# HGRN2 recurrence by halvings for two heads at once, forget and query projections in seven products

## The chip, the cores and the metric

The kernel runs on one core of a Trainium2 chip. The metric is device time in microseconds (us): the median of three runs.

## The reference, cut to what matters

One layer of a trunk on 512 frames of width 1024, in float32. After an RMSNorm `h`, one projection by `w_in` gives eight column groups: `zu`, `zv` (gMLP, 512 each), `zq`, `zf`, `zi`, `zo` (recurrence, 1024 each) and two gates of 1024.

```python
log_f = log_sigmoid(zf); k = sigmoid(-zf); q = silu(zq)       # 8 heads of 128
# S_t = diag(f_t) S_(t-1) + k_t v_t^T ;  o_t = S_t^T q_t, v = zi
o = rmsnorm(o, norm_g) * silu(zo)
mix = sigmoid(g_a) * (gmlp @ w_up_a) + sigmoid(g_b) * (o @ w_up_b)
x = x + mix @ w_out
x = rmsnorm(x + square(relu(rmsnorm(x) @ w_ff1)) @ w_ff2)
```

Within a group of 128 frames the recurrence is a causal 128x128 score matrix per head, score(s, t) = sum over channels of k_s q_t times the product of the f between s and t; across groups a 128x128 state is carried.

## The kernel before

Activations stand transposed: channels on the 128 partitions, 512 frames along the free side. Every large matrix product is done in three passes of float32r: `split` (lines 97 to 99) makes a high half on ScalarE and the rest on VectorE, and `mm3` (115 to 124) issues high x high, high x low, low x high for each 128-row block. `operand` and `wload` (101 to 109) bring a 512 KB weight tile and split it into one of five buffers (`NOPER`). `chan_proj` (299 to 304) is one projection onto 128 channels: 8 blocks x 3 passes, 512 columns each. `tok_proj` (317 to 320) projects onto frames, 256 columns a matmul.

`seven` (126 to 166) computes two neighbouring channel projections together by seven products of half-size blocks (Winograd's form): 4 blocks x 3 passes x 256 columns for each product. It needs sums of weight blocks (`s1` to `s4`, made by VectorE in `S` tiles) and sums of frame quarters, which `frames_operands` (168 to 190) makes and splits. It is used for the gates (line 598) and the first feed-forward layer (679), not for `ZF` and `ZQ`.

Order of the work: norm, `zv` and `zu` with the gMLP; four rounds, each `proj_round` (line 387 on: `ZI` by `tok_proj`, then for two heads `ZF` and `ZQ` by `chan_proj`, with `F`, `K` by two sigmoids and `Q` by sigmoid and product) and then `hgrn_head` for its two heads; `ZO`; `w_up_a`; the operands of the frames; the gates; `w_up_b`; `w_out`; the feed-forward layers.

`hgrn_head` (409 to 542) builds the scores of one head. `cellwise` (413 to 418) multiplies 32x32 cells, four groups of the array's columns in turn; float32, so each matmul is two records in the trace. After the diagonal come two levels of radix 4 (b = 1 and 4, six differences each, kept in widened copies `QX` of Q), then doublings at 16, 32 and 64 in place. Predicated copies merge each level into `cells`; ScalarE copies cells into `scores`. Then the states (`pst`, `st`) and the outputs (`po`), normed with `rstd_of` on GpSimd. The weight transfers are issued by SP; GpSimd issues accumulating transfers in the second feed-forward layer (line 760).

A scheduler orders each engine's instructions at build time from its own estimate of durations; on the chip every engine runs its list in order.

## Time and profile before

| | us |
|---|---|
| median of 3 runs | 835.21 (834.03 to 835.6) |
| profiled execution, its time | 836.09 |
| its span, first to last instruction | 834.2 |
| TensorE busy | 818.7 |
| VectorE busy | 599.2 |
| ScalarE busy | 408.5 |

The profile is one execution. TensorE's busy time overlaps its own matmuls, so it shows whether the engine has work, not its pace. The mean granted clock of TensorE over the span is 0.993 of full speed.

### The profile page before, as it was taken

The numbers are of one execution on the slowest core, as the hardware profiler recorded it, in microseconds if no ns is written. First come the engines' busy times: TensorE is split into PE (matmuls) and PEld (weight loads), VectorE is DVE, ScalarE is ACT, GpSimd is POOL, SyncE is SP. The second block draws the span as 40 slices with busy tenths as digits, with TensorE's granted clock in tenths as the row PEclk, the third lists the DMA queues.
The fourth block names the chain that finished last, engine by engine and source line by source line (L and its number), as shares of the span: only waits on it lengthen the run. The fifth ranks groups of instructions, "written<-read, shape, count | busy, mean of one in ns | idle before, by whom it ended". The sixth has DMA issues, their size and how long they took to land.

```text
span 834.2 us, 15111 instructions
## 1 busy us (share of the span) xinstructions
PE 818.7 (98%) x6226; PEld 730.5 (88%) x6226; DVE 599.2 (72%) x955; ACT 408.5 (49%) x676; POOL 47.1 (6%) x81
## 2 busy tenths in 40 slices
PE   8999999999999999999999999899999999999996
PEld 7989888879789988999878889899999988878884
DVE  7563767676685587887574369777777575899996
ACT  6433434344333345556442343677677652555454
POOL 2000000000000000000000021000000000010103
PEclk9999999999999999999999999899999999999998
DMA  9233321221311212323434411233333396193802
GB/s 337 88 110 106 98 67 68 73 66 40 102 52 52 93 36 76 102 101 103 152 101 173 156 62 41 77 105 120 105 103 101 104 303 176 43 292 99 235 11 101
DMA packets 26919, 92.44 MB, mean 111 GB/s; under 512 B 3489, under 2 KB 3873, under 8 KB 26850
## 3 DMA queue, kind: packets, MB, share of 16 engines
q1 hardware_dynamic: 24546, 84.13, 30.4%
q0 software_dynamic: 1728, 6.29, 4.1%
q8 instruction: 49, 0.80, 0.4%
q10 hardware_dynamic: 576, 1.05, 0.3%
q14 instruction: 20, 0.16, 0.1%
HBM read 89.36 MB, written 2.10 MB: 110 GB/s over the span
## 4 chain that ended last, share of the span: by engine, by line
PE 94%; DVE 2%; ACT 1%; issue 1%; POOL 1%; POOLq 0%; ACTq 0%; DVEq 0%
PE acc L122 15%; PE acc L124 15%; PE acc L123 15%; PE prodx L124 5%; PE prodx L122 5%; PE prodx L123 5%; PE prodzy L123 4%; PE prodzy L124 4%; PE prodzy L122 4%; PE hm L122 3%; PE hm L124 3%; PE hm L123 3%; PE y L122 2%; PE y L124 2%; PE y L123 2%; PE sp L417 2%
## 5 line engine op out<-in xcount | busy, mean ns | idle before, releaser
L99 DVE TENSOR_TENSOR WL<-raw,WH 128x1024 fp32r<-128x1024 f32 (+1 forms) x134 | 151.4, 1134 | 101.4 <-ACT WH L98 100.5
L98 ACT ACTIVATE WH<-raw 128x1024 fp32r<-128x1024 f32 (+1 forms) x134 | 132.2, 989 | 164.6 <-PE acc L123 62.7
L122 PE MATMUL acc<-WH,hTH 128*128 128x256 f32 x320 | 91.5, 286 | 0.0
L124 PE MATMUL acc<-WH,hTL 128*128 128x256 f32 x320 | 91.3, 285 | 0.0
L123 PE MATMUL acc<-WL,hTH 128*128 128x256 f32 x320 | 91.0, 284 | 0.0
L122 PE MATMUL acc<-hTH,WH 128*128 128x512 f32 x160 | 64.2, 401 | 0.0
L124 PE MATMUL acc<-hTH,WL 128*128 128x512 f32 x160 | 64.2, 401 | 0.0
L123 PE MATMUL acc<-hTL,WH 128*128 128x512 f32 x160 | 63.5, 397 | 0.0
L99 DVE TENSOR_TENSOR WL<-s,WH 128x1024 fp32r<-128x1024 f32 x44 | 53.8, 1222 | 10.0 <-ACT WH L98 9.0
L122 PEld LDWEIGHTS acc<-WH,hTH 128*128 128x128 f32 x320 | 60.3, 189 | 0.6
L123 PEld LDWEIGHTS acc<-WL,hTH 128*128 128x128 f32 x320 | 60.3, 188 | 0.5
L124 PEld LDWEIGHTS acc<-WH,hTL 128*128 128x128 f32 x320 | 60.3, 189 | 0.2
L98 ACT ACTIVATE WH<-s 128x1024 fp32r<-128x1024 f32 x44 | 46.7, 1062 | 16.1 <-PE prodx L123 9.5
L123 PE MATMUL hm<-WL,aH 128*128 128x512 f32 x96 | 38.0, 396 | 0.0
L124 PE MATMUL hm<-WH,aL 128*128 128x512 f32 x96 | 38.0, 395 | 0.0
L122 PE MATMUL hm<-WH,aH 128*128 128x512 f32 x96 | 37.9, 396 | 0.0
L124 PEld LDWEIGHTS acc<-hTH,WL 128*128 128x128 f32 x160 | 30.0, 188 | 7.1
L123 PEld LDWEIGHTS acc<-hTL,WH 128*128 128x128 f32 x160 | 30.0, 188 | 6.6
L122 PEld LDWEIGHTS acc<-hTH,WH 128*128 128x128 f32 x160 | 30.0, 188 | 6.5
L98 ACT ACTIVATE WH<-rawx 128x1024 fp32r<-128x1024 f32 x24 | 25.1, 1054 | 19.6 <-issue 10.7
L122 PE MATMUL prodx<-h2H,WH 128*128 128x256 f32 x112 | 31.4, 280 | 1.8 <-ACT WH L98 1.8
L123 PE MATMUL prodzy<-h2L,WH 128*128 128x256 f32 x112 | 32.1, 287 | 0.0
(295 smaller groups left out, 2344.6 us busy)
## 6 DMA issues: line engine op xcount, KB each, us to landing
raw<-in_w_dram SPq DMA_DIRECT2D x128, 512.0 KB, 3.6
rawx<-in_w_dram SPq DMA_DIRECT2D x18, 512.0 KB, 8.5
rawx<-in_w_dram POOLq DMA_DIRECT2D x6, 512.0 KB, 6.6
raw<-in_w_dram POOLq DMA_DIRECT2D x6, 512.0 KB, 8.1
x_t<-in_x_dram SPq DMA_DIRECT2D x4, 512.0 KB, 5.7
x<-in_x_dram SPq DMA_DIRECT2D x4, 512.0 KB, 5.2
out_dram<-x ACTq DMA_DIRECT2D x4, 256.0 KB, 2.8
out_dram<-x SPq DMA_DIRECT2D x4, 256.0 KB, 2.4
```

Source lines behind the costliest of these rows:

```text
L98: nc.scalar.activation(H, src, AF.Copy)
L99: nc.vector.tensor_tensor(L, src, H.bitcast(F32), ALU.subtract)
L122: nc.tensor.matmul(acc, ah, bh, start=first and i == 0, stop=False, **kw)
L123: nc.tensor.matmul(acc, ah, bl, start=False, stop=False, **kw)
L124: nc.tensor.matmul(acc, al, bh, start=False, stop=last and i == n - 1, **kw)
L417: nc.tensor.matmul(sp[p * C:(p + 1) * C, t * n:(t + 1) * n], K[:, t * P + p * C:t * P + (p + 1) * C], x(t, p), start=True, stop=True)
```

## The change

- `ZF` and `ZQ` of a round are each computed for two heads by `seven`, 8 calls in all. There, `s1` and `s3` are made by transfers (a plain one on SP, an accumulating one on GpSimd), `x` lies in the `acc` buffers, and `zy` has one buffer instead of two. One sign is taken out of the sums, so that the second channel half comes out negated; `fin` undoes it with a scale.
- The operands of the frames are made once, ahead of the `zu` projections, in `o_n`'s space, with a copy by ScalarE for the later two frame groups; the gates use the same ones. `n3` has a tile of its own there. In the first feed-forward layer the operations of `frames_operands` stand in another order.
- `hgrn_pair` replaces `hgrn_head`: both heads of a round in one set of tiles, 1024 wide; after the diagonal five halvings (b = 1, 2, 4, 8, 16) and then 32 and 64, Q and K updated in place. `sp` has two buffers instead of four. The outputs stay per head.
- The gMLP result `ya` is kept in float32 and split ahead of `w_up_a`, in space that the recurrence had.
- The masks are smaller, and GpSimd's transfers have a smaller descriptor space.

The core of the diff:

```diff
--- before.py
+++ after.py
-RADIX = [1, 4]
 C = 32
 NC = P // C
-PAIRS = [(1, 1), (2, 1), (3, 1), (2, 2), (3, 2), (3, 3)]
+LEVELS = [1, 2, 4, 8, 16]
...
-    def seven(nameA, nameB, rhs, pool, psum, g, func):
+    def seven(nameA, nameB, rhs, pool, psum, g, fin, dma=False):
...
-        x = ps.tile([P, S], F32, tag="hm", bufs=2, name="prodx")[:, :256]
-        zy = psum.tile([P, 2, S], F32, tag="zy", bufs=2, name="prodzy")
+        xtag = "acc" if dma else "hm"
+        x = ps.tile([P, S], F32, tag=xtag, bufs=2, name="prodx")[:, :256]
+        zy = psum.tile([P, 2, S], F32, tag="zy", bufs=1 if dma else 2, name="prodzy")
...
+        if dma:
+            A1, B = A["w"][index[nameA]][:, :S], A["w"][index[nameB]]
+            for s, more in ((s1, B[:, S:]), (s3, A1)):
+                nc.sync.dma_start(s, B[:, :S])
+                nc.gpsimd.dma_start(s, more, accum_op=ALU.add)
         WA = operand(ra)
         product(x, WA, 0, "11", True, False)
         nc.scalar.copy(u[:, :256], x)
-        nc.vector.tensor_tensor(s1, a21, a22, ALU.add)
-        nc.vector.tensor_tensor(s2, s1, a11, ALU.subtract)
+        if not dma:
+            nc.vector.tensor_tensor(s1, a21, a22, ALU.add)
+        nc.vector.tensor_tensor(s2, s1, a11, ALU.add)
         WS = operand(s12)
-        product(y, WS, 0, "t1", True, False)
+        product(y, WS, 0, "n1", True, False)
         nc.scalar.copy(v, y)
-        product(x, WS, 1, "t2", False, False)
+        product(x, WS, 1, "n2", False, False)
         nc.scalar.copy(u[:, 256:], x)
-        nc.vector.tensor_tensor(s3, a11, a21, ALU.subtract)
-        nc.vector.tensor_tensor(s4, a12, s2, ALU.subtract)
+        if not dma:
+            nc.vector.tensor_tensor(s3, a11, a21, ALU.add)
+        nc.vector.tensor_tensor(s4, a12, s2, ALU.add)
         product(z, WA, 1, "21", True, True)
         WT = operand(s34)
-        product(x, WT, 0, "t3", False, False)
+        product(x, WT, 0, "n3", False, False)
         nc.vector.tensor_tensor(g[:, 1, 256:], x, v, ALU.add)
-        nc.scalar.activation(g[:, 1, 256:], g[:, 1, 256:], func)
+        fin(1, slice(256, S), g[:, 1, 256:])
         product(y, WT, 1, "22", False, True)
         nc.vector.tensor_tensor(g[:, 0, :].rearrange("p (l t) -> p l t", l=2),
                                 u.rearrange("p (l t) -> p l t", l=2), zy[:, :, :256], ALU.add)
-        nc.scalar.activation(g[:, 0, :], g[:, 0, :], func)
-        product(x, operand(a22), 0, "t4", False, True)
-        nc.scalar.activation(g[:, 1, :256], x, func)
-
-    def frames_operands(pool, H, L, tmp):
+        fin(0, slice(0, S), g[:, 0, :])
+        product(x, operand(a22), 0, "n4", False, True)
+        fin(1, slice(0, 256), x)
+    def act_by_sign(g, func):
+        def fin(i, cols, src):
+            nc.scalar.activation(g[:, i, cols], src, func, scale=-1.0 if i else 1.0)
+        return fin
+    def frames_operands(pool, H, L, tmp, own3=False, have=()):
         q = {f"{j + 1}{l + 1}": (H[:, 4 * j:4 * j + 4, 256 * l:256 * l + 256],
...
         for n in ("11", "21", "12", "22"):
-            nc.vector.tensor_tensor(x[n], q[n][0].bitcast(F32), q[n][1].bitcast(F32), ALU.add)
+            if n not in have:
+                nc.vector.tensor_tensor(x[n], q[n][0].bitcast(F32), q[n][1].bitcast(F32), ALU.add)
         out = {n: q[n] for n in ("11", "21", "22")}
-        out["t3"] = q["12"]
-        for n in ("t1", "t2", "t4"):
+        out["n3"] = q["12"]
+        for n in ("n1", "n2", "n4") + (("n3",) if own3 else ()):
             out[n] = tuple(pool.tile([P, 4, 256], F32R, name=f"{n}{p}") for p in "HL")
-        t1, t2, t3, t4 = x["11"], x["22"], x["12"], x["21"]
-        nc.vector.tensor_tensor(t1, x["12"], x["11"], ALU.subtract)
-        split(t1, *out["t1"])
-        nc.vector.tensor_tensor(t3, x["22"], x["12"], ALU.subtract)
-        nc.vector.tensor_tensor(t2, x["22"], t1, ALU.subtract)
-        split(t2, *out["t2"])
-        split(t3, *out["t3"])
-        nc.vector.tensor_tensor(t4, x["21"], t2, ALU.subtract)
-        split(t4, *out["t4"])
+        n2, n4, n1, n3 = x["11"], x["21"], x["12"], x["22"]
+        nc.vector.tensor_tensor(n3, x["22"], x["12"], ALU.subtract)
+        if own3:
+            split(n3, *out["n3"])
+        nc.vector.tensor_tensor(n1, x["11"], x["12"], ALU.subtract)
+        split(n1, *out["n1"])
+        nc.vector.scalar_tensor_tensor(n2, n3, -1.0, x["11"], ALU.mult, ALU.subtract)
+        split(n2, *out["n2"])
+        if not own3:
+            split(n3, *out["n3"])
+        nc.vector.scalar_tensor_tensor(n4, x["21"], -1.0, n2, ALU.mult, ALU.subtract)
+        split(n4, *out["n4"])
         return out
...
+    hT = o_n.rearrange("p t d -> p (t d)").rearrange("p (k s) -> p k s", k=KD)
+    hq = [hT[:, 4 * j:4 * j + 4, 256 * l:256 * l + 256] for j in range(2) for l in range(2)]
...
-    yaH = pya.tile([P, NG, S], F32R, name="yaH")
-    yaL = pya.tile([P, NG, S], F32R, name="yaL")
+    ya = pya.tile([P, NG, S], F32, name="ya")
...
+            if t >= 2:
+                nc.scalar.copy(hT[:, 4 * half:4 * half + 4, t * P:(t + 1) * P], pt)
...
+    rhs = frames_operands(ph, hTH, hTL, hq, True, ("12", "22"))
...
-        y = gp.tile([P, S], F32, tag="y", bufs=2, name="y")
-        nc.vector.tensor_tensor(y, m.rearrange("p n q -> p (n q)"), u, ALU.mult)
-        split(y, yaH[:, g, :], yaL[:, g, :])
+        nc.vector.tensor_tensor(ya[:, g, :], m.rearrange("p n q -> p (n q)"), u, ALU.mult)
...
+    scores = [hg.tile([P, 2, NT, P], F32, name=f"scores{i}") for i in range(2)]
+    cells = [hg.tile([P, 2, NT, C], F32, name=f"cells{i}") for i in range(2)]
...
-        heads = []
...
+        F, K, Q = (hg.tile([P, 2, S], F32, tag=n, bufs=2, name=f"{n}{r}") for n in "FKQ")
+        def fin_f(i, cols, src):
+            nc.scalar.activation(K[:, i, cols], src, AF.Sigmoid, scale=1.0 if i else -1.0)
+            nc.scalar.activation(F[:, i, cols], src, AF.Sigmoid, scale=-1.0 if i else 1.0)
+        def fin_q(i, cols, src):
+            sq = hg.tile([P, S], F32, tag="sq", bufs=1, name="sq")[:, cols]
+            nc.scalar.activation(sq, src, AF.Sigmoid, scale=-1.0 if i else 1.0)
+            nc.vector.scalar_tensor_tensor(Q[:, i, cols], src, -1.0 if i else 1.0, sq, ALU.mult, ALU.mult)
+        for z, g, fin in ((ZF, F, fin_f), (ZQ, Q, fin_q)):
+            seven(("chan", z + 256 * r), ("chan", z + 256 * r + 128), rhs, hg, ps_sc, g, fin, True)
+        return V, F, K, Q
+    def hgrn_pair(r, V, F, K, Q0):
+        sc, cl = scores[r % 2], cells[r % 2]
+        def flat(x):
+            return x.rearrange("p h t -> p (h t)")
+        def cellwise(sp, x, n, of=1):
+            for h in range(2):
+                for t in range(NT):
+                    for p in range(0, NC, of):
+                        c0 = t * P + p * C
+                        nc.tensor.matmul(sp[p * C:(p + 1) * C, (h * NT + t) * n:(h * NT + t + 1) * n],
+                                         K[:, h, c0:c0 + C], x(h, c0), start=True, stop=True)
+        def bank(name):
+            return ps_sc.tile([P, S], F32, tag="sp", bufs=2, name=f"sp{r}_{name}")
+
+        sp = bank(0)
+        cellwise(sp, lambda h, c0: Q0[:, h, c0:c0 + C], C)
+        Q = hg.tile([P, 2, S], F32, tag="QF", bufs=2, name=f"QF{r}")
+        nc.vector.tensor_tensor(flat(Q), flat(Q0), flat(F), ALU.mult)
+        nc.vector.copy_predicated(cl.rearrange("p h t c -> p (h t) c"),
+                                  mask[0][:, None, :].broadcast_to([P, 2 * NT, C]),
+                                  sp[:, :2 * NT * C].rearrange("p (n c) -> p n c", c=C))
+
+        T = flat(F)
+        def double(b, T):
+            n = 2 * S // (2 * b)
+            T2 = T.rearrange("p (g i) -> p g i", i=2)
+            Tn = hg.tile([P, n], F32, tag=f"T{b}", bufs=1, name=f"T{b}_{r}")
+            nc.vector.tensor_tensor(Tn, T2[:, :, 0], T2[:, :, 1], ALU.mult)
+            for x, i in ((K, 0), (Q, 1)):
+                xv = flat(x).rearrange("p (g i b) -> p g i b", i=2, b=b)[:, :, i, :]
+                nc.vector.tensor_tensor(xv, xv, T2[:, :, 1 - i, None].broadcast_to([P, n, b]), ALU.mult)
+            return Tn
+        for b in LEVELS:
+            sp = bank(b)
+            cellwise(sp, lambda h, c0: Q[:, h, c0:c0 + C].rearrange("p (g i b) -> p g i b", i=2, b=b)[:, :, 1, :], 16)
+            T = double(b, T)
+            nc.vector.copy_predicated(
+                cl.rearrange("p h t (g i b) -> p (h t) g i b", i=2, b=b)[:, :, :, 1, :],
+                mask[b][:, None, :].broadcast_to([P, 2 * NT, 16]).rearrange("p n (g b) -> p n g b", b=b),
+                sp[:, :2 * NT * 16].rearrange("p (n g b) -> p n g b", n=2 * NT, b=b))
+        for p in range(NC):
+            nc.scalar.copy(sc[p * C:(p + 1) * C, :, :, p * C:(p + 1) * C], cl[p * C:(p + 1) * C])
+        sp = bank(C)
+        cellwise(sp, lambda h, c0: Q[:, h, c0 + C:c0 + 2 * C], C, 2)
+        for p in range(0, NC, 2):
+            nc.scalar.copy(sc[p * C:(p + 1) * C, :, :, (p + 1) * C:(p + 2) * C],
+                           sp[p * C:(p + 1) * C, :2 * NT * C].rearrange("p (h t c) -> p h t c", h=2, t=NT))
+        T = double(C, T)
+        sp = bank(64)
+        for h in range(2):
+            for t in range(NT):
+                nc.tensor.matmul(sp[0:64, (h * NT + t) * 64:(h * NT + t + 1) * 64], K[:, h, t * P:t * P + 64],
+                                 Q[:, h, t * P + 64:(t + 1) * P], start=True, stop=True)
+        nc.scalar.copy(sc[0:64, :, :, 64:128], sp[0:64].rearrange("p (h t c) -> p h t c", h=2, t=NT))
+        T = double(64, T)
+        for h in range(2):
+            outputs(2 * r + h, V, K[:, h, :], Q[:, h, :], sc[:, h], T[:, h * NT:(h + 1) * NT])
+    def outputs(h, V, K, Q, sc, Tt):
         hc = slice((h % 2) * P, (h % 2 + 1) * P)
...
-        V, heads = cur
-        for hd in heads:
-            hgrn_head(V, *hd)
+        hgrn_pair(r, *cur)
...
+    left2 = ExitStack()
+    pu = left2.enter_context(tc.tile_pool(name="pu", bufs=1, side="left", reuse_waits="tile"))
+    yaH = pu.tile([P, NG, S], F32R, name="yaH")
+    yaL = pu.tile([P, NG, S], F32R, name="yaL")
+    for g in range(0, NG, 2):
+        split(ya[:, g:g + 2, :], yaH[:, g:g + 2, :], yaL[:, g:g + 2, :])
...
+    left2.close()
...
-    rhs = frames_operands(pt, hTH, hTL, [part[1][:, 2 * i:2 * i + 2, :].rearrange("p d (l t) -> p (d l) t", l=2)
-                                         for i in range(4)])
...
-            seven(("chan", c0 + 128 * d), ("chan", c0 + 128 * d + 128), rhs, pt, ps_g, g, AF.Sigmoid)
+            seven(("chan", c0 + 128 * d), ("chan", c0 + 128 * d + 128), rhs, pt, ps_g, g, act_by_sign(g, AF.Sigmoid))
...
-    nc = _bacc.Bacc("TRN2", target_bir_lowering=False, num_devices=1)
+    nc = _bacc.Bacc("TRN2", target_bir_lowering=False, num_devices=1, dynamic_dma_scratch_size=4096)
```

## Rows read from the trace of the kernel before

**Rows 1.** The page: busy time of each engine, and the chain that ended last
```profile
PE 818.7 (98%) x6226; PEld 730.5 (88%) x6226; DVE 599.2 (72%) x955; ACT 408.5 (49%) x676; POOL 47.1 (6%) x81
...
PE 94%; DVE 2%; ACT 1%; issue 1%; POOL 1%; POOLq 0%; ACTq 0%; DVEq 0%
```

**Rows 2.** Busy us (instructions) in stretches, granted clock, DMA share
```profile
24.00:65.50 41.50, 41.50 (x263) 37.11 (x261) 25.18 (x38) 15.26 (x21) 3.23 (x8) 1.00 0.28 90
65.50:302.00 236.50, 236.50 (x2571) 207.69 (x2570) 156.06 (x420) 93.07 (x221) 13.13 (x20) 1.00 0.23 72
302.00:326.30 24.30, 22.59 (x112) 18.54 (x110) 21.24 (x26) 12.05 (x18) 0.00 (x0) 1.00 0.22 65
326.30:404.00 77.70, 77.68 (x654) 77.44 (x655) 62.83 (x78) 47.54 (x80) 0.00 (x0) 1.00 0.34 108
...
526.00:533.00 7.00, 6.36 (x31) 6.08 (x30) 4.92 (x6) 4.28 (x9) 0.00 (x0) 0.52 0.40 129
```

**Rows 3.** Waits of TensorE, longest first: total, times, longest
```profile
PE prodx L122 <- ACT WH L98: 2.7, 2, 1.8
```

**Rows 4.** Timeline of TensorE, 44 to 72: first and last of 21 matmuls
```profile
46.38 0.40 PE L122 MATMUL acc<-hTH,WH 128*128 128x512 f32 x1
...
51.05 0.39 PE L124 MATMUL acc<-hTH,WL 128*128 128x512 f32 x1
```

**Rows 5.** Timeline of TensorE, 326 to 372: first and last of 36 matmuls
```profile
329.15 0.28 PE L122 MATMUL prodx<-t2H,WH 128*128 128x256 f32 x1
...
333.27 0.28 PE L124 MATMUL prodzy<-hTH,WL 128*128 128x256 f32 x1
```

**Rows 6.** Chain that ended last, 99 to 126: start, us, what
```profile
99.53 0.77 PE sp L417 x62
...
104.40 0.48 PE sp L417 x32
...
108.15 0.38 PE sp L417 x32
108.52 0.31 PE acc L124
...
111.91 0.38 PE sp L417 x16
...
117.62 0.61 PE sp L512 x8
```

**Rows 7.** Groups of VectorE: busy us, mean ns | idle before
```profile
L99 DVE TENSOR_TENSOR WL<-raw,WH 128x1024 fp32r<-128x1024 f32 x112 | 136.4, 1222 | 101.1 <-ACT WH L98 100.4
...
L147 DVE TENSOR_TENSOR s<-raw 128x512 f32<-128x512 f32 x22 | 15.2, 690 | 0.6 <-DMA raw<-in_w_dram 0.2
...
L491 DVE TENSOR_TENSOR Q<-Q,T 128x256 f32<-128x256 f32 x24 | 10.0, 418 | 0.0
L463 DVE TENSOR_TENSOR QX<-QX,F 128x128 f32<-128x128 f32 x24 | 9.6, 423 | 0.0
...
L463 DVE TENSOR_TENSOR Q<-QX,T 128x128 f32<-128x128 f32 x24 | 5.9, 288 | 3.6 <-PE po L536 3.5
...
L429 DVE COPY_PREDICATED cells<-mask,sp 128x128 f32<-128x128 int32 x8 | 2.4, 298 | 1.5 <-PE sp L417 1.4
```

**Rows 8.** Groups of ScalarE: busy us, mean ns | idle before
```profile
L98 ACT ACTIVATE WH<-raw 128x1024 fp32r<-128x1024 f32 x112 | 118.3, 1059 | 141.9 <-PE acc L123 60.9 <-PE acc L124 19.5 <-PE y L123 19.3
```

**Rows 9.** Timeline of TensorE, 323 to 328, with idle time before
```profile
325.06 0.39 PE L122 MATMUL prodx<-hTH,WH 128*128 128x256 f32 x1 [0.97 <-ACT WH L98]
...
326.32 0.38 PE L124 MATMUL prodx<-hTH,WL 128*128 128x256 f32 x1 [0.76 <-DVE WL L99]
```

**Rows 10.** Timeline of TensorE, 522.5 to 534
```profile
525.69 0.38 PE L122 MATMUL prodx<-h2H,WH 128*128 128x256 f32 x1 [1.75 <-ACT WH L98]
```

**Rows 11.** The page: DMA issues, us from issue to landing
```profile
raw<-in_w_dram SPq DMA_DIRECT2D x128, 512.0 KB, 3.6
...
raw<-in_w_dram POOLq DMA_DIRECT2D x6, 512.0 KB, 8.1
```

More of the change, by code (lines that the diff above doesn't have):

```diff
@@ L57, in _plan @@
         names += [("tok", ZI + 256 * r, k) for k in (0, 1)]
-        for h in (2 * r, 2 * r + 1):
-            names += [("chan", ZF + 128 * h), ("chan", ZQ + 128 * h)]
+        names += [("chan", z + 128 * h) for z in (ZF, ZQ) for h in (2 * r, 2 * r + 1)]
     for g in range(4):
@@ L253, in trunk_kernel @@
     hTL = ph.tile([P, KD, S], F32R, name="hTL")
+    hT = o_n.rearrange("p t d -> p (t d)").rearrange("p (k s) -> p k s", k=KD)
+    hq = [hT[:, 4 * j:4 * j + 4, 256 * l:256 * l + 256] for j in range(2) for l in range(2)]
     right3 = ExitStack()
     pya = right3.enter_context(tc.tile_pool(name="pya", bufs=1, side="right"))
-    yaH = pya.tile([P, NG, S], F32R, name="yaH")
-    yaL = pya.tile([P, NG, S], F32R, name="yaL")
-    shift(pya)
+    ya = pya.tile([P, NG, S], F32, name="ya")
     left = ExitStack()
@@ L374, in trunk_kernel @@
     nc.sync.dma_start(hng, A["hg_norm_g"].rearrange("o v -> v o"))
-    mask = []
-    for b in (0, *RADIX, 16):
-        n = {0: C, 16: 16}.get(b, 6 * C // 4)
-        m = hg.tile([P, NT * n], I32, name=f"mask{b}")
-        nc.sync.dma_start(m, A[f"mask{b}"])
-        mask.append(m)
-    scores = [hg.tile([P, NT, P], F32, name=f"scores{i}") for i in range(2)]
-    cells = [hg.tile([P, NT, C], F32, name=f"cells{i}") for i in range(2)]
+    mask = {}
+    for b in (0, *LEVELS):
+        mask[b] = hg.tile([P, 16 if b else C], I32, name=f"mask{b}")
+        nc.sync.dma_start(mask[b], A[f"mask{b}"])
+    scores = [hg.tile([P, 2, NT, P], F32, name=f"scores{i}") for i in range(2)]
+    cells = [hg.tile([P, 2, NT, C], F32, name=f"cells{i}") for i in range(2)]
     for sc in (*scores, *cells):
@@ L393, in proj_round @@
         tok_proj(ZI + 256 * r, evac_v)
-        heads = []
-        for h in (2 * r, 2 * r + 1):
-            zf = chan_proj(ZF + 128 * h)
-            F = hg.tile([P, S], F32, tag="F", bufs=3, name=f"F{h}")
-            K = hg.tile([P, S], F32, tag="K", bufs=3, name=f"K{h}")
-            nc.scalar.activation(F, zf, AF.Sigmoid)
-            nc.scalar.activation(K, zf, AF.Sigmoid, scale=-1.0)
-            zq = chan_proj(ZQ + 128 * h)
-            Q = hg.tile([P, S], F32, tag="Q1", bufs=2, name=f"Q1_{h}")
-            sq = hg.tile([P, S], F32, tag="sq", bufs=2, name=f"sq{h}")
-            nc.scalar.activation(sq, zq, AF.Sigmoid)
-            nc.vector.tensor_tensor(Q, zq, sq, ALU.mult)
-            heads.append((h, F, K, Q))
@@ L678, in trunk_kernel @@
         g = acts[f // 8][:, f % 8:f % 8 + 2, :]
-        seven(("ff1", f), ("ff1", f + 1), rhs, pq, ps_f, g, AF.Relu)
+        seven(("ff1", f), ("ff1", f + 1), rhs, pq, ps_f, g, act_by_sign(g, AF.Relu))
         nc.scalar.activation(g, g, AF.Square)
@@ L863, in _mask @@
     import numpy as np
-    s = np.arange(P) % C
-    if b == 0:
-        m = (s[:, None] == np.arange(C)).astype(np.int32)
-    elif b == 16:
-        m = np.repeat((s < 16)[:, None], 16, axis=1).astype(np.int32)
-    else:
-        m = np.zeros((P, C // (4 * b), len(PAIRS), b), np.int32)
-        for g in range(C // (4 * b)):
-            for x, (i, d) in enumerate(PAIRS):
-                m[:, g, x, :] = (s // b == 4 * g + i - d)[:, None]
-    return np.tile(m.reshape(P, -1), (1, NT))
+    s = np.arange(P)[:, None] % C
+    if b:
+        m = s // b == 2 * (np.arange(16)[None, :] // b)
+    else:
+        m = s == np.arange(C)[None, :]
+    return m.astype(np.int32)
 def kernel(**inputs):
@@ L889 @@
         "wsT": i["gmlp_ws"][0].transpose(2, 0, 1),
-        **{f"mask{b}": _mask(b) for b in (0, *RADIX, 16)},
+        **{f"mask{b}": _mask(b) for b in (0, *LEVELS)},
         "gmlp_ln_g": i["gmlp_ln_g"][0],
```

88 lines of the change are left out of this document (removed).

## Prediction

> **What bounds the kernel now.** I read the page first: TensorE is busy for 98% of the span and holds 94% of the chain that ended last; VectorE stands at 72% [rows 1]. An average can hide stages with other limits, so next the windows: in the long stretch from 65.5 to 302 us, where the recurrence lies, TensorE is busy for all of 236.50 us while VectorE is at 156.06 and ScalarE at 93.07 [rows 2]. Last the waits of TensorE: the largest entry of the whole span is 2.7 us [rows 3]. So the time is the sum of what TensorE issues plus a few microseconds of gaps. A busy TensorE row does not show its pace, since matmuls overlap in the records; the pace is the distance between starts, and I take that from the timeline.
>
> **Projections: the gain.** ZF and ZQ are 16 projections of 24 matmuls with 512 columns. Undisturbed, 21 of them start in 4.67 us, 0.2335 each [rows 4]. The gate stage already runs the seven-product form: 36 of its 256-column matmuls start in 4.12 us, 0.1177 each [rows 5]. Two projections cost 48 x 0.2335 = 11.21; one `seven` costs 7 x 4 x 3 = 84 x 0.1177 = 9.89. Gain 1.32, eight times: **-10.6 us**, all of it on the engine that sets the end. That `seven` keeps TensorE fed is seen in the gates: 77.68 busy of 77.70, with VectorE at 62.83 [rows 2].
>
> **Recurrence on TensorE: a loss.** Before, a head issues, by the chain's own pieces, 0.77 for the diagonal and first radix level together, 0.48 for the second radix level, 0.38 for b=16, 0.38 for the 32-level (16 records), 0.61 for the 64-level: 2.62, so 5.24 for two heads [rows 6]. Each record is half of a matmul, so 16 cells are 32 records. After, a pair issues the diagonal and five halvings, six bursts of 64 records, then 32 and 16 records for the last two. No row shows 64 records of 16 columns. Upper bound: every 64 cost the 0.77 of 62 wider ones: 6 x 0.77 + 2 x 0.38 + 2 x 0.61 = 6.60. Lower bound: a longer burst shares its start; 30 records more cost 0.77 - 0.48 = 0.29, so a 16-column burst of 64 is 0.38 + 0.31 = 0.69, and with 0.6 and 1.0 for the last two the pair is 0.77 + 5 x 0.69 + 1.6 = 5.8. The matmul behind a burst holds the chain for 0.31 instead of 0.12 [rows 5, 6]; ten such places become eight, -0.38 at most, and nothing where bursts follow each other already. A pair thus costs +0.2 to +1.4 more, four pairs +0.8 to +5.4; I take **+3.0**, the middle.
>
> The rows put 62 records in 0.77 us, 12.4 ns each [rows 6]. The Trainium skill ("TensorE: Matmul & The Clock Gate", "Wait — 56ns, not 53.3ns?") says that starts never come closer than about 25 ns, however narrow the matmul. The trace disagrees where four column groups take turns; by the Trainium skill's figure this step would be, as an estimate, 128 more records a pair x 25 ns x 4 = +12.8 instead of +3.0. The 32-level, which uses two column groups, does take 0.38 for 16 records, 24 ns [rows 6].
>
> **VectorE: no net change.** Prices: 1.22 for 1024 elements, 0.69 for 512, 0.42 for 256, 0.29 for 128 and 0.42 for 128 with strided operands, 0.30 for a predicated copy of 128 [rows 7]. Recurrence before, per head: one of 512, ten of 256, thirteen of 128, eight predicated copies and six tiny ones of some 0.2: 0.69 + 4.2 + (3.8 to 5.5) + 2.3 + 1.2 = 12.2 to 13.9, so 24 to 28 a pair. After, a pair: Q times F 1.22; fourteen in-place products of 512, 9.7; seven T products, 0.69 + 0.42 + 0.29 + four of about 0.2 = 2.2; predicated copies 0.43 + 5 x 0.30 = 1.9: 15.0, and up to 17.5 if the strided price (0.13 more per 128) holds for every short stride at b=1 and 2. So about -10 a round. Projections before: four operands and two Q products, 4 x 1.22 + 2 x 0.69 = 6.3. After: two sevens, each three 1024 operands, one of 512, s2 and s4, the sums of 256 and 512 = 3.67 + 0.69 + 1.38 + 1.1 = 6.84, and three Q pieces 1.5: 15.2, +8.9. VectorE stays near 156 us in a stage of about 229: two thirds, less than in the gates. ScalarE gains two sevens' splits and copies and loses score copies; from 93 it may go to about 110 of 229. Both lie beside TensorE at 0. If VectorE's cover failed, a late operand costs TensorE that operand's 1.06 + 1.22 [rows 7, 8].
>
> The chain of a pair: eight levels of a burst (0.8) and two products (1.4) with hand-overs of about 0.5, some 22 us, then the outputs of two heads, which are unchanged. On TensorE, ZI and ZO are 96 x 0.1177 = 11.3 each and the 16 projections 89.7, which leaves 56 of the 236.50 us for eight heads and the start of w_up_a: at most 7 a head. A round after is then 11.3 + 19.8 + some 14 = 45 us, so the chain fits; the last pair has the four ZO projections, 45 us, over it.
>
> **Frame operands: moved.** Now they are made around the window from 302 us, VectorE at 21.24 of 24.30, and TensorE loses 0.97 + 0.76 there [rows 2, 9]. What it waits for is a seven's WA; I infer that the second seven's was put ahead because the first one's next operand was not ready. With operands ready long before, TensorE takes the first seven in order: **-1.7**. Early, they cost VectorE ten operations of 1.22 less four of 0.69 for ya: +9.4 on 25.18 of 41.50 [rows 2]; ScalarE +6 on 15.26. They are due at the first seven's second product, about 78 us, after the ZI projection; hidden. If not, the same 1.7 comes back there. The split of ya, 1.06 + 1.22, lies behind ZO if the last recurrence ends before ZO does; else TensorE pays up to 2.3 ahead of w_up_a, since yaH lies where the recurrence's tiles were.
>
> **DMA.** Each seven in a round adds two plain loads of 256 KB on SP and two accumulating ones on POOL. Rows: 3.6 us for 512 KB on SP, 8.1 for an accumulating one [rows 11]; 32 more transfers, 8.4 MB, in a stage where the DMA engines are at 0.23 [rows 2]. Queued behind s12's and s34's loads on SP are the next raw tiles; behind the waiting accumulate on POOL is `rstd` of a head, whose PSUM tile the next head's output needs. Hidden at 0 if early; the cost otherwise is the second rival. Smaller masks and subtractions turned into additions cost the same as before: 0. The smaller scratch for POOL's transfers could delay the twelve accumulates of the last stage; I take 0, and the 8.1 of one landing [rows 11] is the most that a late one would cost.
>
> **First feed-forward layer.** Its operands follow another order (n3 ahead of n1): one operation, 1.22, later or, if the order of readiness decides, none. Now TensorE waits 1.75 there for ScalarE's WH [rows 10], and the granted clock of the next 7 us is 0.52, the lower level of 1.2 GHz for nearly all of it: 31 matmuls in 7.00 us that take 3.65 at full pace, 3.4 lost [rows 2]. The order written out may shift that either way: -5.2 if the wait goes, +1.2 if it grows. I take 0.
>
> **Sum.** 836.1 - 10.6 + 3.0 - 1.7 = 826.8 for the profiled execution, which lies 0.9 above the median of the three runs; against the median 835.2 - 9.3 = **826 us**. Its own range from the bounds (burst price, a few waits of 1 to 2 us) is 822.5 to 830.
>
> **Rivals.**
> *Rounds partly starved.* In a round one seven no longer interleaves with another as in the gates: `zy` has one buffer, `sp` two instead of four. If planned and real lateness differ by 1 us at each of the eight sevens, up to 6 us return: 830 to 833.5. For it: VectorE and DMA waits now sit in a static order. Against: TensorE has no gap at all in that stretch before [rows 2].
> *Slower: the sums of weight blocks come late.* s12 of ZQ needs the buffer that ZF's split releases, then 3.6 + 8.1 for two transfers (512 KB rows), 0.69 for s2, 1.06 + 1.22 for the split: 14.7. From that release to the use lie, if WS is split four products ahead, 9.9 + 4 x 1.41 = 15.5. A margin under 1 us: if an accumulate lands 3 us later than that, TensorE stands for 2 us at each ZF-to-ZQ step. A wait of 1.75 has cost 3.4 more in clock [rows 2, 10]; four such steps are 22 less the gain of 9: about 848; if the clock falls at two of them only, 841. It decides from a wait of 1.75 us a step on if the clock falls, from 2.8 if it holds. Against: 256 KB should land sooner than 512, and TensorE has bursts of the previous pair to fill with.
> *No gain.* If the 128 records that a pair gains cost the 24 ns each of the two-group level, the recurrence takes 4 x 128 x 0.024 = +12.3 instead of +3.0 and the sum is 835.2 - 10.6 + 12.3 - 1.7 = 835. Four column groups at 12.4 ns speak against it. The Trainium skill's floor (same section) would give this case.
> *More than forecast.* The wait and the lower clock in the feed-forward layer vanish: 826 - 5 = 821.
>
> **Chances.** Forecast 0.58, rounds partly starved 0.12, more than forecast 0.12, no gain 0.08, slower 0.10. A measurement of this kernel tells about 0.2%, 1.7 us, from no change. Faster is 0.58 + 0.12 + 0.12 = 0.82, same 0.08, slower 0.10. The range 820 to 834 leaves out the slower case, most of no gain and the best end.
>
> **What would show it.** Right: 256-column matmuls at 0.118 apart in the rounds, no TensorE wait over 1 us between 66 and 300, bursts of 64 records near 0.7, VectorE near 156 in that stage, no wait at the first gate. Wrong: TensorE waiting for DMA, for WL of an s tile or for `zy` in the rounds; granted clock below 1.00 there; bursts of 64 records above 1.2; PE idle ahead of w_up_a.

## The result, and the profile after

The changed kernel takes **846.88 us**, median of 4 runs (843.47 to 847.34), against 835.31 for the kernel before in the same comparison: ratio 1.013, 95% interval 1.0106 to 1.0155. It is slower, by more than the gain that was forecast. All times below are of fast executions; the one slow execution, 843.69 us of e24, is left out. The profiled execution took 847.13 us, span 845.4, mean granted clock 0.986.

The page of the changed kernel, busy time:

```profile
PE 816.9 (97%) x7026; PEld 744.2 (88%) x7026; DVE 597.8 (71%) x811; ACT 421.5 (50%) x686; POOL 63.8 (8%) x97
```

Beside [rows 1] the sums hardly moved. The windows of the changed kernel tell where the time is (columns as in [rows 2]):

```profile
67.00:130.00 63.00, 60.05 (x849) 58.71 (x848) 36.68 (x56) 26.82 (x45) 8.40 (x11) 1.00 0.47 128
130.00:190.00 60.00, 55.98 (x848) 52.72 (x847) 42.75 (x77) 29.21 (x67) 6.11 (x8) 0.97 0.42 105
190.00:299.00 109.00, 109.00 (x1640) 104.27 (x1639) 71.86 (x138) 44.67 (x104) 8.82 (x12) 1.00 0.30 90
299.00:309.00 10.00, 4.62 (x26) 3.60 (x24) 5.11 (x9) 5.37 (x13) 1.27 (x2) 0.69 0.16 53
309.00:338.70 29.70, 28.73 (x130) 23.43 (x128) 13.22 (x18) 8.39 (x13) 0.00 (x0) 0.87 0.12 36
```

Three places: TensorE idles for 7 us between 67 and 190, where before it had no gap [rows 2]; from 299 to 309 it is busy for 4.62 of 10 us; and `w_up_a`, right behind, runs at a granted clock of 0.87 (the lower level, 1.2 GHz, for part of it). The waits of TensorE from 60 to 330 us name the releasers:

```profile
PE sp L437 <- DVE QF L463: 4.6, 2, 2.6
PE py L566 <- DVE o_n L521: 3.1, 1, 3.1
PE po L514 <- ACT hjunk L518: 2.6, 4, 1.2
PE acc L121 <- DVE yaL L97: 1.0, 1, 1.0
```

Before, the longest wait in the same stretch was 1.0:

```profile
PE prodx L122 <- ACT WH L98: 1.0, 1, 1.0
```

The first one is VectorE's fault only at first sight; VectorE's own waits from 66 to 310 us:

```profile
...
DVE s L155 <- DMA s<-in_w_dram: 18.9, 6, 5.3
...
DVE s L155 <- issue: 5.2, 1, 5.2
```

VectorE stands in its list at `s2` (line 155) until an accumulating transfer has landed, and the pair's products behind it stand too. In order of time, one such place, first on VectorE and then on TensorE:

```profile
131.59 0.69 DVE L155 TENSOR_TENSOR s<-s,raw 128x512 f32<-128x512 f32 x1 [5.18 <-issue]
...
132.80 0.68 DVE L463 TENSOR_TENSOR QF<-QF,T 128x512 f32<-128x512 f32 x1
```
```profile
133.54 0.64 PE L437 MATMUL sp<-QF,K 128*32 128x32 f32 x28 [2.64 <-DVE QF L463]
```

The page's DMA issues (KB each, median us to landing) price the transfers:

```profile
s<-in_w_dram SPq DMA_DIRECT2D x16, 256.0 KB, 3.0
s<-in_w_dram POOLq DMA_DIRECT2D x16, 256.0 KB, 5.2
```

The timeline of TensorE shows the tail: ZO's last matmul, the last head's output products one by one, each behind ScalarE's square of the one before, then transposes that wait for `o_n`, and `w_up_a` at last:

```profile
299.03 0.28 PE L122 MATMUL acc<-WH,hTL 128*128 128x256 f32 x1
299.15 0.38 PE L514 MATMUL po<-V,scores 128*128 128x128 f32 x2
299.37 0.60 PE L566 MATMUL py<-ident,o_n 128*128 128x128 f32 x4
301.20 0.49 PE L514 MATMUL po<-V,scores 128*128 128x128 f32 x2 [1.23 <-ACT hjunk L518]
...
304.37 0.64 PE L516 MATMUL po<-st,QF 128*128 128x128 f32 x2
308.12 1.12 PE L566 MATMUL py<-ident,o_n 128*128 128x128 f32 x4 [3.12 <-DVE o_n L521]
308.89 1.20 PE L120 MATMUL acc<-yaH,WH 128*128 128x512 f32 x2
```

Before, the last output product was out early and `w_up_a` followed ZO at once:

```profile
293.96 0.39 PE L536 MATMUL po<-st,Q 128*128 128x128 f32 x2
...
298.80 0.40 PE L122 MATMUL acc<-yaH,WH 128*128 128x512 f32 x1
```

For an account I add, over the trace's TensorE records from 24 us to `w_up_a`'s last matmul, the time from each start to the next, by kind (a wait is booked on the record ahead of it, so the hole at 305 us counts as outputs). "End" is the start of `w_up_a`'s last matmul. "Large" is all projections, sevens and `w_up_a`; "outputs" are `pk`, `pst`, `po`; all times are us. The other kernels are explained below; from f3 on all have early frame operands and a mended tail, f3 neither sevens nor halvings.

```
                     end    large  bursts  outputs  other
before             323.7    249.4    23.2     21.3    5.8
changed            338.7    252.6    25.7     28.0    8.2
f3  neither        323.7    250.4    23.2     21.2    4.8
b5  sevens         330.3    250.3    24.6     26.7    4.8
b6  halvings       330.4    252.8    25.2     23.6    4.8
e17 both           326.2    246.3    25.7     24.5    5.6
e22 both, sums of rounds 0 and 1 by VectorE
                   323.9    243.4    26.2     24.3    6.0
```

With the gain whole, the large ones of the changed kernel would take 249.4 - 10.6 = 238.8, and 1.4 more for twelve matmuls of the gates that are issued this early: 240.2. 252.6 stand there, so 12.4 us of waits and lower clock ate the gain. The bursts cost 2.5 more, the outputs 6.7, the rest 2.4: with rounding +15.0 at the end of `w_up_a`. The span grew by 11.2, so some 4 us come back behind it.

### The profile page after: what moved, and what is told of

Its sections match the earlier page's. It is cut to its first block, busy times and chain, and to the rows that moved or that the text cites. A ratio compares the mean times of both kernels' runs of the same rounds, so it can differ in the third digit from the quotient of the medians.

```text
span 845.4 us, 16705 instructions
## 1 busy us (share of the span) xinstructions
PE 816.9 (97%) x7026; PEld 744.2 (88%) x7026; DVE 597.8 (71%) x811; ACT 421.5 (50%) x686; POOL 63.8 (8%) x97
## 4 chain that ended last, share of the span: by engine, by line
PE 55%; issue 1%; ACT 1%; DVE 1%; POOL 0%; POOLq 0%; ACTq 0%; DVEq 0%
PE prodx L120 5%; PE prodx L122 5%; PE prodx L121 5%; PE acc L120 5%; PE acc L121 5%; PE acc L122 5%; PE prodzy L122 4%; PE prodzy L120 4%; PE prodzy L121 4%; PE hm L121 3%; PE hm L120 3%; PE hm L122 3%; PE y L120 2%; PE y L122 2%; PE y L121 2%
## 5 line engine op out<-in xcount | busy, mean ns | idle before, releaser
L97 DVE TENSOR_TENSOR WL<-s,WH 128x1024 fp32r<-128x1024 f32 x60 | 73.1, 1222 | 22.0 <-ACT WH L96 16.3
L96 ACT ACTIVATE WH<-s 128x1024 fp32r<-128x1024 f32 x60 | 63.7, 1062 | 37.4 <-PE prodx L121 11.5
L155 DVE TENSOR_TENSOR s<-s,raw 128x512 f32<-128x512 f32 x30 | 20.6, 686 | 24.1 <-DMA s<-in_w_dram 18.9
L120 PE MATMUL prodzy<-hTH,WH 128*128 128x256 f32 x128 | 36.2, 283 | 0.3 <-ACT u L158 0.3
L121 PE MATMUL prodzy<-hTL,WH 128*128 128x256 f32 x128 | 36.0, 281 | 0.0
L122 PE MATMUL prodzy<-hTH,WL 128*128 128x256 f32 x128 | 36.0, 281 | 0.0
L120 PE MATMUL prodx<-n2H,WH 128*128 128x256 f32 x120 | 34.5, 288 | 1.0 <-ACT u L152 1.0
L120 PE MATMUL prodx<-n4H,WH 128*128 128x256 f32 x120 | 33.9, 283 | 0.3 <-DVE Q L167 0.3
L122 PE MATMUL prodx<-n2H,WL 128*128 128x256 f32 x120 | 34.1, 284 | 0.0
L121 PE MATMUL prodx<-n2L,WH 128*128 128x256 f32 x120 | 33.9, 283 | 0.0
```

The lines of the kernel that those rows point to most:

```text
L96: nc.scalar.activation(H, src, AF.Copy)
L97: nc.vector.tensor_tensor(L, src, H.bitcast(F32), ALU.subtract)
L120: nc.tensor.matmul(acc, ah, bh, start=first and i == 0, stop=False, **kw)
L121: nc.tensor.matmul(acc, ah, bl, start=False, stop=False, **kw)
L122: nc.tensor.matmul(acc, al, bh, start=False, stop=last and i == n - 1, **kw)
L155: nc.vector.tensor_tensor(s2, s1, a11, ALU.add)
```

## The experiments

The theories at the start: A, the sums of weight blocks come late; B, the last pair ends too late for ZO to cover it; C, narrower PSUM buffers. After the first four runs B was sharpened to E: the order of TensorE's list, with two waits in it, makes the tail. Rivals F to K are named in the expectations.

**e1, sums by VectorE.** Edit in `seven`, for all calls:

```diff
-        if dma:
-            A1, B = A["w"][index[nameA]][:, :S], A["w"][index[nameB]]
-            for s, more in ((s1, B[:, S:]), (s3, A1)):
-                nc.sync.dma_start(s, B[:, :S])
-                nc.gpsimd.dma_start(s, more, accum_op=ALU.add)
...
-        if not dma:
-            nc.vector.tensor_tensor(s1, a21, a22, ALU.add)
+        nc.vector.tensor_tensor(s1, a21, a22, ALU.add)
...
-        if not dma:
-            nc.vector.tensor_tensor(s3, a11, a21, ALU.add)
+        nc.vector.tensor_tensor(s3, a11, a21, ALU.add)
```

> The changed kernel, with s1 and s3 of the rounds made by VectorE (two additions of 0.69 us per seven) instead of a plain and an accumulating transfer; all else as it is. Theory A, late sums: in the changed kernel VectorE stands some 24 us in the rounds ahead of s2, because the accumulate has not landed, and the recurrence queued behind it comes late. Then these waits go, TensorE's gaps between 100 and 140 us (some 7 us, and 1.7 us of lower clock) go with them, and the last pair ends earlier: 830 to 836 us. Theory B, the pair's chain: the last pair takes about 60 us from its first burst to its last output whatever the sums do, and only the ZO projections lie over it: the rounds may gain, the hole of about 9 us at 299 to 309 us and the lower clock after it stay: 838 to 842. Theory C, the narrower PSUM buffers (one zy, two sp): 845 or more.

845.14 us (843.22 to 847.2), ratio 1.011 (1.0076 to 1.0145). The gaps before 140 us went, others came at 163 to 187 us with 6.8 us of half clock, and the tail stayed. A as the whole cause falls.

**e5, ZI behind the sevens in round 3.**

```diff
-        tok_proj(ZI + 256 * r, evac_v)
+        if r < 3:
+            tok_proj(ZI + 256 * r, evac_v)
...
+        if r == 3:
+            tok_proj(ZI + 256 * r, evac_v)
```

> The changed kernel, but in the fourth round alone ZI comes behind the two sevens, so that 11.3 us more of projections lie over the last pair's recurrence. Theory B: the hole ahead of w_up_a (some 8 us without work) and the fall of the clock behind it (13.7 us at the lower level, some 4 to 7 us lost) shrink or go: 835 to 838 us. Theory A: the last pair is late because sums are late in the rounds; the rounds keep their gaps of about 9 us, and the cover takes only what is left: 838 to 842. Theory C: the waits are on buffers and stay: 845 or more.

843.87 us (838.91 to 844.87), 1.0088 (1.0061 to 1.0115). The last output product came 3 us earlier, the hole stayed.

**b1, the kernel before with `hgrn_pair` alone; b2, the changed kernel with the old `hgrn_head`.** The diff of the change, one half at a time (b2 with two `sp` and two `QX` buffers).

> The kernel before, with the recurrence by pairs and halvings alone (projections one by one, operands of the frames at the gates, four sp buffers). Theory B: the hole between ZO and w_up_a appears here too, since two heads now end together: 835 + 3.5 for more bursts + 5 to 12 = 843 to 850 us. Theories A and C: no seven in the rounds, so no late sums and no narrow PSUM: 835 + 3.5 = 837 to 840.

> The changed kernel with the recurrence of before (head by head, radix 4, two sp buffers, two QX buffers instead of three), so the sevens in the rounds with sums by transfers, and the early operands, without the pairwise recurrence. Theory A: VectorE stands for the sums as in the changed kernel and TensorE shows gaps in the rounds: 831 to 837 us. Theory B: heads end one by one as before, no hole ahead of w_up_a: 824 to 828 us. Theory C: the narrow sp and zy buffers show as gaps too: above 835.

b1 845.03 us (844.2 to 847.18), 1.0112 (1.0083 to 1.0142); b2 846.79 (843.2 to 848.39), 1.0136 (1.0103 to 1.0168). Each half alone costs all that the whole costs, so the halves do not add. Both, and e1 and e5, have the wait of 3.1 us for `o_n`. b2 lies above all that A and B had forecast for it; C's "above 835" allows it, and no run gives the sevens four `sp` buffers, so C was not tested by itself.

TensorE's list explains the common wait. `py` for the first heads needs an `hm` buffer of PSUM, and in the order that the scheduler wrote, it stands behind the last head's `po`, which holds one until `o_n` is out; all of `w_up_a` stands behind that `py` (72 of its 96 matmuls in b1). In the changed kernel and b2 its operand `yaH` also lies in space that the recurrence frees last. The kernel before has most of `w_up_a` behind such a `py` too (84 of 96, from 301.6 on), and it cost nothing there, because `o_n` was out in time.

**e14, the transposes in another PSUM pool; e12, also `ya` split early.** e14 has the last line, e12 all (room from one buffer for F and Q):

```diff
-    ya = pya.tile([P, NG, S], F32, name="ya")
+    yaH = pya.tile([P, NG, S], F32R, name="yaH")
+    yaL = pya.tile([P, NG, S], F32R, name="yaL")
...
-        nc.vector.tensor_tensor(ya[:, g, :], m.rearrange("p n q -> p (n q)"), u, ALU.mult)
+        nc.vector.tensor_tensor(u, m.rearrange("p n q -> p (n q)"), u, ALU.mult)
+        split(u, yaH[:, g, :], yaL[:, g, :])
...
-        py = ps.tile([P, NT, P], F32, tag="hm", bufs=2, name="py")
+        py = ps.tile([P, NT, P], F32, tag="acc" if h < 4 else "hm", bufs=2, name="py")
```

> The changed kernel, with only the PSUM buffers of the first four heads' transposes moved from the pool that also holds the last head's output products (hm) to the pool of w_up_a's accumulators (acc); ya is still split when the recurrence's space is released. Theory E (an order with two waits makes the tail: the transposes wait 3.1 us for the last head's PSUM buffer, and w_up_a waits for a split of ya that lies in the space of the recurrence): the 3.1 us wait goes and w_up_a moves up by about as much, but it still starts behind the last output product, so 842 to 845 us. Rival F (the recurrence as a whole is late, and whatever stands behind it waits for it): the wait takes another name in the same place and the time stays at 846 to 848.

> As the run with the transposes in acc, and besides ya is split where it is made, as in the kernel before (room for it: one buffer instead of two for F and for Q). Theory E: w_up_a starts when ZO ends (near 299 us instead of 309), the last head's output products lie between its matmuls, no half clock near 303 to 317; it ends 9 to 11 us earlier than in the changed kernel, and the time is 836 to 839. Rival F: w_up_a starts early, but the gates then wait for what the late recurrence held up, and the time is 843 or more.

e14 845.53 us (841.03 to 849.73), 1.0132 (1.0088 to 1.0177), between the two forecasts: the wait took another name. Its waits of TensorE from 290 to 330 us:

```profile
PE acc L121 <- DVE yaL L97: 3.9, 1, 3.9
PE acc L120 <- ACT yaH L96: 1.5, 1, 1.5
```

e12 837.42 us (834.18 to 842.81), 1.0032 (1.0008 to 1.0055): 9.5 below the changed kernel, as E expected, and `w_up_a` starts at 299.5. Both waits had to go: with the first alone mended (e14), or with `ya` early alone (b1), the hole stays. One new wait came, TensorE from 60 to 75 us:

```profile
PE acc L120 <- ACT u L380: 3.0, 1, 3.0
```

**b4, b1 with `py` in `acc`.**

> The kernel before with the pairwise halvings alone (845 us earlier), and the first four heads' transposes in acc. Its ya was always split early. Theory E: the gap of 3.4 us behind the last output product and the half clock that follows it go, 838 to 841 us, what is left over the kernel before being the bursts (+3.5) and a later start of the gates. Rival F: 845, the wait only takes another name.

843.74 us (842.69 to 846.29), 1.0116 (1.009 to 1.0142). The wait for `o_n` went, but inside `w_up_a` TensorE waited 4.9 us for ScalarE's copies to `part`: ScalarE stood at a split of the gates' weights whose sum VectorE, busy with late frame operands, had not made. Rival F is nearer here. With early frame operands (b6) that wait is 1.0.

**e17, e12 with the product written over `m` instead of `u`.**

> The kernel with ya split early and the transposes in acc (837.4 us), in which a new wait of 3 us stood near 67 us (the gMLP gate's u was held until its split was done); here the product is written over m instead of u. The wait near 67 us and the half clock behind it go: 832.5 to 835 us by theory E, with the gaps near 114 and 134 us still there (theory A). If that wait only moves, 837.

833.37 us (830.7 to 835.56), 0.9989 (0.9975 to 1.0003): as expected, level with before. TensorE's timeline where the hole was, ZO's last matmul first:

```profile
296.63 0.28 PE L122 MATMUL acc<-WH,hTL 128*128 128x256 f32 x1
296.75 0.39 PE L120 MATMUL acc<-yaH,WH 128*128 128x512 f32 x1
296.97 0.40 PE L121 MATMUL acc<-yaL,WH 128*128 128x512 f32 x1
297.21 0.38 PE L517 MATMUL po<-V,scores 128*128 128x128 f32 x2
297.35 0.48 PE L122 MATMUL acc<-yaH,WL 128*128 128x512 f32 x1
...
307.25 0.50 PE L120 MATMUL acc<-yaH,WH 128*128 128x512 f32 x1 [0.99 <-ACT part L553]
```

**e16, e12 with the edits of e1 and e5.**

> As the run before it, and besides s1 and s3 are summed by VectorE instead of by accumulating transfers, and in the last round the value projection ZI stands behind the two seven-product projections. Theory E with theory A (late sums make the gaps of the first rounds, 9 us of gaps and half clock): all three causes gone but for the gaps that the sums by VectorE showed near 163 to 187 us; 828 to 833 us, below the kernel before. Rival F: 840 or more. A third outcome, 834 to 839, would say that the rounds' gaps move rather than go.

838.28 us (836.82 to 839.3), 1.0041 (1.0027 to 1.0055). The third outcome: the gaps of the rounds moved.

**e18, e17 with `s1` and `s3` by GpSimd** (e1's edit with `nc.gpsimd`, so the gates' and the first feed-forward layer's sums too).

> As the run with m, and s1 and s3 are summed by GpSimd out of the two loaded blocks instead of by accumulating transfers. Theory A (the sums by transfer come late and starve the first rounds): the gaps near 110 to 140 us go and, since VectorE has no more to do than in the changed kernel, none comes at 163 to 187 us: 829 to 832 us, below the kernel before. Rival H (VectorE's and ScalarE's queues, not the sums, make the rounds' gaps, or GpSimd is too slow for the sums): gaps of 3 us or more stay in the rounds, 834 or more.

846.92 us (846.42 to 847.45), 1.0153 (1.0137 to 1.0168). The page, group of GpSimd's `s1`, and the durations of VectorE's `s2` (min/median/max ns):

```profile
L148 POOL TENSOR_TENSOR s<-raw 128x512 f32<-128x512 f32 x30 | 54.5, 1816 | 249.5 <-DVE WL L97 156.1
```
```profile
L149 DVE TENSOR_TENSOR s<-s,raw x30: 672/1666/1793, 54.3 to 655.3; 128x512 f32<-128x512 f32 x30
```

GpSimd takes 1.82 us for a sum, and VectorE's sum grows from a median of 0.69 us (e17) to 1.67. So this run says nothing on A. With ZI last as well (e19) it was 841.53 (840.62 to 845.72), where 827 to 830 had been expected.

**f1, the kernel before with early frame operands alone** (`frames_operands` ahead of `zu`, `hT` kept, `ya` split late, as in the diff of the change; with them comes the other order of operands in the first feed-forward layer, here and in f3, b5 and b6).

> The kernel before with the early frame operands alone (ya split late, hT kept), its projections and its recurrence unchanged. Theory E: the late split of ya costs nothing while the recurrence ends ahead of ZO, as it does here (last output product 294 us, ZO's end 299): w_up_a starts within 1 us of ZO's end, 834 to 837 us. Rival G (the late split alone makes the hole): a hole of 3 us or more and a half clock, 839 to 843.

832.84 us (831.53 to 834.32), 0.9986 (0.9975 to 0.9997). No wait for `ya` stands in its trace, and the longest of TensorE from 60 to 330 us is 1.0: the late split is free when the recurrence ends ahead of ZO.

**f3, b5, b6: a two by two with e17.** All have early frame operands, `ya` split early over `m`, `py` in `acc`; b5 adds the sevens to f3, b6 the halvings, e17 is both. The buffers go with them: b5 and e17 have two `sp` and one `zy`, b5 two `QX` instead of three, b6 and e17 one buffer for F and for Q.

> The corner of a two by two without sevens and without halvings: the kernel before with early frame operands (832.8 us so far), ya split early over m, and the transposes in acc. Both theories: 830 to 834, as there is no hole to mend here.

> The corner with the seven-product projections (sums by transfer) and the recurrence of the kernel before, with the tail mended in the same three ways. Theory E (the tail alone hid the gain): the sevens' 10.6 us come through less a few us of gaps in the first rounds, 823 to 828, below both kernels. Rival J (the rounds give the gain back: late sums, two PSUM buffers instead of four for the scores): 830 or more, gaps of 6 us or more before 200 us.

> The corner with the pairwise halvings and the old projections, tail mended, frame operands early. Theory E: base plus the bursts' 3.5 us and the last pair's longer chain, 835 to 838. Rival J (the pair's chain is the trouble, mended or not): 840 or more. With the changed kernel so mended at 833.4, the sevens' worth beside the pair is 833.4 minus this.

f3 **831.21 us** (830.96 to 832.29), 0.9963 (0.9948 to 0.9977); b5 836.74 (836.16 to 837.27), 1.0033 (1.002 to 1.0046); b6 838.86 (838.32 to 840.32), 1.0059 (1.0044 to 1.0074). By the ratios, times 835: the sevens cost 5.8 us beside the old recurrence and gain 5.8 beside the halvings; the halvings cost 8.0 beside the old projections. Rival J holds for b5: TensorE waits for the heads' products in the rounds, and its half clock lies from 134.0 to 140.8 us. TensorE's first wait in b5, 60 to 330 us, and what VectorE did ahead of the longest:

```profile
PE sp L439 <- DVE K L494: 5.8, 3, 3.2
```
```profile
132.93 0.69 DVE L156 TENSOR_TENSOR s<-s,raw 128x512 f32<-128x512 f32 x1 [5.16 <-DMA s<-in_w_dram]
```

So the longest stands behind a late sum, as in the changed kernel. f3 is below both kernels, and e17 is 2.2 above f3: with the tail mended the two halves together still gain nothing.

**e22, e17 with transfers only in rounds 2 and 3** (VectorE sums in rounds 0 and 1); **b5h, the same on b5; e24, e22 with ZI last in round 3.**

> The mended changed kernel (833.4 us) with the sums of rounds 0 and 1 by VectorE, and those of rounds 2 and 3 by accumulating transfer. Theory A (in the first rounds VectorE has room and the transfers come late; later it is the other way round): the gaps near 107 to 135 us go and none comes at 163 to 187: 829 to 831.5. Rival H (VectorE's queue is the limit in either case): 833 or more, with gaps of the same sum elsewhere.

> The corner with sevens and the recurrence of the kernel before (836.7 us; gaps of 1.9 and 3.5 us near 111 and 132 us and a half clock of 6.8 us behind them), with the sums of rounds 0 and 1 by VectorE. Theory A: these gaps and the half clock go, 7 to 9 us: 828 to 830. Rival J (two PSUM buffers instead of four and the pair's late start, not the sums): 834 or more.

> The mended changed kernel with the sums of rounds 0 and 1 by VectorE (835.9 us, its profiled run 832.5), and in the last round ZI behind the two seven-product projections. Theory E, continued (after the mending, the last pair's chain still ends 10 us behind ZO's end and stretches w_up_a by some 5 us; an earlier start of the chain takes that back): the last output product 4 us or more earlier, 829 to 832. Rival K (PE was full there and the chain cost only its own matmuls): within 1.5 us of 835.9, or of the run's lower end.

e22 835.94 us (831.8 to 840.02), 1.0022 (0.9999 to 1.0045); b5h 834.32 (832.24 to 839.01), 1.0005 (0.9986 to 1.0024), 2.4 below b5, as rival J expected; e24 833.36 (830.09 to 840.41), 0.9997 (0.9974 to 1.002), its last output product at 305 us, not earlier than e22's at 303. In e22's profile no two starts of the rounds are more than 1.3 us apart, yet the median is not below e17's. These kernels scatter: e24's times of 830.09 and 830.1 come with a granted clock of 0.997, that of 840.41 with 0.986, while f3 stays within 1.3 us at 0.997 to 0.998. In which stretch the long executions lose their clock was not seen.

## Why the prediction was wrong, point by point

**The gain of 10.6.** Right as a price: in the rounds 256-column matmuls start 0.118 apart (22 of them in 2.48 us from 214.01 in the changed kernel). It did not come out whole anywhere: by the account, against f3's 250.4, e22 keeps 7.0 of it, e17 4.1, the changed kernel none. And e22, with no two starts of its rounds more than 1.3 us apart, still does not end `w_up_a` ahead of f3: bursts take 3.0 more there, outputs 3.1, the rest 1.2.

**The bursts, +3.0.** Right: 23.2 to 25.7 us, and 64 records of 16 columns take 0.74, as here in the changed kernel:

```profile
262.75 0.74 PE L437 MATMUL sp<-QF,K 128*32 128x16 f32 x64
267.40 0.74 PE L437 MATMUL sp<-QF,K 128*32 128x16 f32 x64
272.04 0.70 PE L437 MATMUL sp<-QF,K 128*32 128x32 f32 x32
277.00 1.15 PE L487 MATMUL sp<-QF,K 128*64 128x64 f32 x16
281.25 0.49 PE L499 MATMUL pk<-ident,K 128*128 128x128 f32 x3
```

That is 11.6 ns a record, so the rival *no gain* falls. The Trainium skill ("TensorE: Matmul & The Clock Gate", "Wait — 56ns, not 53.3ns?") says that starts are never closer than about 25 ns; where four column groups take turns this trace disagrees.

**The failed step** is "some 22 us, then the outputs of two heads, which are unchanged", with "the last pair has the four ZO projections, 45 us, over it", and with it the bound "else TensorE pays up to 2.3 ahead of w_up_a". In the changed kernel the last pair's first burst is at 242.2 and its last output product at 304.6: 62 us, and ZO ends at 299.0. The levels take 36 us of it instead of 22, the outputs 24. A level takes 4.6 us, since its burst stands in TensorE's list some 2.5 us behind the point at which VectorE has its operand (QF is out at 264.83, the burst is at 267.40). Yet against the kernel before that is not what made it late: the last burst begins at 277.0, before at 276.4. The outputs did. Before, one head's outputs were left then, 280.5 to 294.3; now both heads' are, one behind the other, 281.3 to 305.0. I had counted their work, which is unchanged, and not that they now lie in a row behind the last level. It is not the only way to be late: b2 has one head's outputs left, as before, but its last burst begins at 289.5 and its last output product at 304.3.

What that lateness cost was set by two things: the order with `py` ahead of `w_up_a`, which I had not priced, and the operand of `w_up_a` in space freed last, which I had priced at 2.3 at most. `w_up_a` starts 9.9 us behind ZO's end, and the clock behind the hole is at 1.2 GHz for part of it; "PE idle ahead of w_up_a" was on my own list of signs. With these mended, and one buffer instead of two for F and Q to make room, 846.9 became 833.4 (e12, e17). That the mending must take both is shown by e14 and b1; that the late split alone is harmless, by f1.

The mending explains 13.5 us. What is left from 833.4 to the forecast 826 is the second failed term, a gain of 10.6 "all of it on the engine that sets the end": of the 10.6 the account shows 4.1 in e17.

**The sums.** "VectorE: no net change" held as an average (151.3 us busy from 67 to 299, against 156.06 [rows 2]). But it stood 24 us at `s2`. The rival *the sums of weight blocks come late* named 841 to 848 us and got the time, for the wrong reason in the main: without late sums the time was still 845.1 (e1), though VectorE's extra work brought gaps of its own there. In the mended kernels early sums in rounds 0 and 1 gain 2.4 us beside the old recurrence and nothing that the scatter lets one see beside the new (e22 against e17).

**The gates' wait, -1.7.** A third of it: at the first gate two starts stood 1.36 and 1.04 us after the one before; they stand 1.31 and 0.53 after it in the changed kernel, 1.36 and 0.52 in f1. One of 0.8 is left in f3, with `ya` early and `py` moved. My inference that late frame operands caused the wait is borne out for the second at most, not for the first.

**The first feed-forward layer, taken as 0.** It gained. The wait of 1.75 [rows 10] stands in every trace with the old order (b1 and b4 too) and is 0.9 in the changed kernel, f1, f3 and b6, so it goes with the order of the operands. Before, the granted clock was at half for 6.8 us there; in f3 it is full:

```profile
520.00:534.00 14.00, 12.41 (x104) 12.00 (x103) 13.17 (x17) 9.99 (x18) 0.00 (x0) 1.00 0.29 82
```

But the clock does not follow from that wait alone. With the same wait of 1.75, b1 has its clock reduced and b4 not, and the changed kernel, with the shorter one, has it reduced too (0.79 from 536 to 544); the windows of b1 and b4:

```profile
537.00:545.00 8.00, 7.05 (x44) 6.85 (x45) 6.10 (x6) 5.10 (x10) 0.00 (x0) 0.79 0.39 124
```
```profile
535.00:543.00 8.00, 7.12 (x58) 6.92 (x59) 7.09 (x8) 5.16 (x11) 0.00 (x0) 1.00 0.37 126
```

f3's 3.5 us lie in the shorter waits here and at the gates and in the clock; how much is the clock's stays open. So "has cost 3.4 more in clock" was true of one execution and is no price of such a wait.

The rival *rounds partly starved* (830 to 833.5) is what e17 came to, once the tail was mended.

**Still open** is why the sevens cost beside the old recurrence (b5). Sums by transfer are some 2.4 of it; two score buffers instead of four, one `zy` and both heads' Q arriving at once remain, not tried apart.

## What to carry to other kernels

A price for work moved off the critical engine is worth only as much as the cover at the end of its stage: ask when the last piece ends, in the lists as they are ordered, and what stands behind it in the same list, the same PSUM buffers and the same memory. Two units made into one save nothing at the end if their last steps then lie in a row. When two halves of a change each cost what the whole costs, look for one place that both run into, mend it, and measure the halves again.

## What the runs showed of the hardware

GpSimd and VectorE slow each other in sums of two SBUF operands (e18). One sum on each engine with the other idle, then two that overlap:

```profile
63.69 1.27 POOL L148 TENSOR_TENSOR s<-raw 128x512 f32<-128x512 f32 x1 [5.94 <-DVE WL L97]
65.00 0.69 DVE L149 TENSOR_TENSOR s<-s,raw 128x512 f32<-128x512 f32 x1 [1.39 <-POOL s L148]
```
```profile
69.30 1.68 POOL L155 TENSOR_TENSOR s<-raw,raw 128x512 f32<-128x512 f32 x1 [4.34 <-DVE WL L97]
69.74 1.79 DVE L156 TENSOR_TENSOR s<-raw,s 128x512 f32<-128x512 f32 x1
```

Over the run VectorE's median became 1.67 and GpSimd's mean 1.82. The Trainium skill ("GPSIMD Engine Reference", "8. Key points") says that they share the SBUF interfaces where VectorE reads two SBUF inputs; this trace agrees. A transfer of 256 KB that accumulates, issued by GpSimd, lands 5.2 us after its issue (median), a plain one issued by SP 3.0.
